# A hybrid decoder trunk on one core: VectorE adds, a plain pair in block 1, stores and adaLN pieces in another order

## The chip, the cores and the metric

The kernel runs on 1 core of one Trainium2 chip. The metric is the device time of one execution in microseconds (us). Before the change it is 2479.21 us, the median of 3 runs (2479.11 to 2483.68). Engines are named as in the profile: PE is TensorE (PEld its weight loads), DVE is VectorE, ACT is ScalarE, POOL is GpSimd, SP is SyncE, which issues the transfers.

## The reference

The kernel computes one inference step of a four-layer trunk for a prompt of 1024 tokens and for 8 samples of 4 tokens, all with width 1024 in float32. Layer 0 and layer 3 are gated short convolutions, layer 1 is an RG-LRU block, layer 2 differential attention. Each layer takes a shift, scale and gate from a conditioning vector (adaLN), and ends with a residual and a LayerNorm. The change touches the two convolution layers and the order of adaLN work:

```python
def adaln(c, w, b):
    m = (jax.nn.silu(c) @ w + b)[:, None, :]
    shift, scale, gate = jnp.split(m, 3, axis=-1)

def short_conv_mixer(u, buf, w_in, conv_w, w_out):
    h, bg, cg, z = jnp.split(u @ w_in, 4, axis=-1)
    y, new_buf = causal_dwconv(cg * h, buf, conv_w)      # width 3
    return (jax.nn.silu(z) * bg * y) @ w_out, new_buf
```

## The kernel before, in words

Prompt and sample tokens stand side by side: NT = 1056 columns, features on the 128 partitions, so an activation is 8 tiles of 128 x 1056. Every float32 operand of a large product is split into a high and a low part (`split`, L93 and L94: ACT casts the high part, DVE subtracts), and a product is three matmuls per block of 128 features. Unit `u[k]` holds both parts of input block k; `y[k]` is where the layer's output will stand, and until then it is used for other things.

The input projection of a convolution layer has four parts (q = 2: cg, 0: h, 3: z, 1: bg), each with 8 column blocks i. `conv_layer` makes them in three ways.

- Block 0 is made plainly, in three chunks of 384, 384 and 288 columns (`part`, with `gemm_chunk`, L124), 24 matmuls a chunk and part. Its results are multiplied, convolved and gated by ACT and DVE, and stored to `yd[0]` by three stores (L496), issued as they are traced.
- Blocks 1 to 7 are made in pairs of two parts: kind 0 is cg and h, kind 1 is z and bg. A pair (`pair`, matmuls at L603) takes seven products of half width instead of eight, 7 x 24 matmuls of 264 columns. It needs sums of the inputs and of the weights. `conv_sums` makes the input sums for four pairs of blocks d: two adds of 128 x 1056 on POOL (L393), which join the high and low part of `u[d]` and `u[d + 4]`, four subtractions of 528 columns on DVE (L397 to L400), and two splits into `y[d]` and `y[d + 4]`. The sums are traced by `more()` between block 0's parts; their tiles come from a ring of three. `conv_pair_weights` makes a pair's weights in six stages: load, direct (a split of the first weight), sums, early, late, last. The stages of the next pair are traced inside the current one; those of the first pair, block 1 kind 0, all ahead of it, after `swap(True)` has closed block 0's pool of temporaries and opened the pool of the fast form.
- The last pair, block 7 kind 1, is plain again (L690, 2 x 4 chunks of 264 columns), with weights from `conv_weights`.

Full plain weights live in a ring of two slots (`wtile`), and the raw loads in another ring of two (`raw`); in layer 0 the fast form has raw tiles of its own. In layer 0 the plain weights of block 0 are slots 1 and 2 of the ring and `y[2]`, `y[3]`; in layer 3 one of them is `y[1]`.

The adaLN projection of a layer is six pieces (`ada_piece`, L186 to L208): four loads of 512 KB into the raw ring, 8 matmuls of 512 columns, an ACT copy, four transposes, two DVE instructions. `filler(s, tot)` traces the pieces that are due at step s: in layer 0 the gate of layer 0 (two pieces) and the six of layer 1, in layer 1 those of layers 2 and 3.

The order on each engine isn't the traced one. A planner runs a simulated time line over the traced program and puts each instruction on its engine when its inputs and memory are ready there; earlier traced instructions go first. Each engine, and the SP queue of transfers, then works through its own list in order.

Of the kernel before, what the change touches and what calls it, by code (L numbers as in the profile page):

```python
# [14 lines left out]
AF = mybir.ActivationFunctionType  # L15
# [30 lines left out]
class Trunk:  # L46
# [340 lines left out]
    def conv_sums(self, l, u, e, d):  # L387
        nc = self.nc
        b = []
        for x in (u[d], u[d + 4]):  # L390
            t = self.xct(f"cs{l}_{d}_{len(b)}")
            xf = x.bitcast(F32)
            nc.gpsimd.tensor_tensor(t, xf[:, :NT], xf[:, NT:], ALU.add)  # L393
            b.append(t)
        (b11, b12), (b21, b22) = ((t[:, :HB], t[:, HB:]) for t in b)
        tt = nc.vector.tensor_tensor
        tt(b11, b12, b11, ALU.subtract)  # L397
        tt(b12, b22, b12, ALU.subtract)
        tt(b22, b22, b11, ALU.subtract)
        tt(b21, b21, b22, ALU.subtract)  # L400
        for t, o in zip(b, (e[d], e[d + 4])):
            self.split((o[:, :NT], o[:, NT:]), t, NT)
# [55 lines left out]
    def conv_layer(self, l, u, y, filler, wts, swap, yd):  # L458
# [10 lines left out]
        def part(i, q, c, wt, cg, yc, sz, p, psv):  # L469
            c0, n = CH[c]  # L470
            npr = min(n, T - c0)
            ps = self.gemm_chunk(wt, u, c, f"in{l}_{i}_{q}_{c}")
            if q == 2:
                cg[c] = cg.get(c) or self.sm(f"cg{l}_{i}_{c}")
                nc.scalar.copy(cg[c][:, :n], ps[:, :n])
            elif q == 0:
                yc[c] = yc.get(c) or self.sm(f"yc{l}_{i}_{c}")
                t = p[c] = self.sm(f"p{l}_{i}_{c}")
                if c == 0:
                    nc.gpsimd.memset(t[:, 0:2], 0.0)  # L480
                else:
                    nc.gpsimd.tensor_copy(t[:, 0:2], p[c - 1][:, 384:386])
                nc.vector.tensor_tensor(t[:, 2 : 2 + npr], ps[:, :npr], cg[c][:, :npr], ALU.mult)
                if npr < n:
                    nc.vector.tensor_tensor(
                        psv[:, :, 2:6], ps[:, npr:n].rearrange("p (b t) -> p b t", b=NB),
                        cg[c][:, npr:n].rearrange("p (b t) -> p b t", b=NB), ALU.mult,
                    )
                conv(i, t, yc[c], psv, npr, n)
            elif q == 3:  # L490
                sz[c] = sz.get(c) or self.sm(f"sz{l}_{i}_{c}")
                nc.scalar.activation(sz[c][:, :n], ps[:, :n], AF.Silu)
            else:
                nc.vector.tensor_tensor(sz[c][:, :n], ps[:, :n], sz[c][:, :n], ALU.mult)
                nc.vector.tensor_tensor(yc[c][:, :n], yc[c][:, :n], sz[c][:, :n], ALU.mult)
                nc.sync.dma_start(yd[i][:, c0 : c0 + n], yc[c][:, :n])  # L496


        def conv(i, t, o, psv, npr, n):
# [20 lines left out]
            return psv  # L520


        sums = [0, 1, 2, 3] if first else [0, 2, 3, 1]

        def more():
# [5 lines left out]
        if first:  # L531
            for s in range(4):
                ld(s)
            for c in range(3):
                for s, q in enumerate((2, 0, 3, 1)):
                    part(0, q, c, wts[s], cg, yc, sz, p, psv)
                    if c == 2:
                        more()
            for s in range(4):
                filler(s, 4 * KB)  # L540
        else:
            for s in range(3):
                ld(s)
            for c in range(3):
                for s, q in enumerate((2, 0)):
                    part(0, q, c, wts[s], cg, yc, sz, p, psv)
            for s in range(2):
                wts.pop(s)
            ld(3)
            for s, q in ((2, 3), (3, 1)):  # L550
                if s == 2:
                    for c in range(3):
                        sz[c] = self.sm(f"sz{l}_0_{c}")
                for c in range(3):
                    more()
                    part(0, q, c, wts[s], cg, yc, sz, p, psv)
        wts.clear()
        swap(True)


# [30 lines left out]
        def pair(i, kind, get, o, stages, fills):  # L591
# [3 lines left out]
            for n, (tgt, mov) in enumerate(steps):  # L595
# [16 lines left out]
                elif n == 2:  # L612
                    u2 = copies(f"u2{nm}", B["X"])
                elif n == 3:
                    p5 = copies(f"p5{nm}", B["Z"])
                elif n == 4:
                    u3 = copies(f"u3{nm}", B["X"])
                    for jj in range(2):
                        nc.gpsimd.tensor_tensor(u3[jj], u3[jj], p5[jj], ALU.add)  # L619
                elif n == 5:  # L620
                    for jj in range(2):
                        nc.vector.tensor_tensor(
                            o[:, HB + QH * jj : HB + QH * jj + QH], B["Z"][jj][:, :QH], u2[jj], ALU.add)
# [3 lines left out]
                    filler(fills.pop(0), 4 * KB)  # L627
            return [t[:, :QH] for t in B["X"]] + u3

        self.deal(tp="Q", mm="U", a="P", b="R")  # L630
        todo = [(i, k) for i in range(1, KB) for k in range(2)][:-1]
        stages, get = self.conv_pair_weights(l, *todo[0], raw)
        for f in stages:
            f()
        yc = None
        for n, (i, kind) in enumerate(todo):
            w2 = {}
            if n + 1 < len(todo):
                stages, nxt = self.conv_pair_weights(l, *todo[n + 1], raw)
            else:  # L640
                def wl(s):
                    return lambda: w2.update({s: self.conv_weights(l, y, s)})
                stages, nxt = [lambda: None, wl(4 * KB - 2), lambda: None, lambda: None, lambda: None, wl(4 * KB - 1)], None
            fills = [4 * i + 2 * kind, 4 * i + 2 * kind + 1]
            if kind == 0:
                t = wide(f"cp{l}_{i}")
                nc.gpsimd.memset(t[:, 0:2], 0.0)
                psv = past(i)
                o = t[:, 2 : NT + 2]
            else:  # L650
                t = wide(f"sz{l}_{i}")
                o = t[:, :NT]
            second = pair(i, kind, get, o, stages, fills)
            if kind == 1:
                for h in range(2):
                    nc.scalar.activation(o[:, HB * h : HB * h + HB], o[:, HB * h : HB * h + HB], AF.Silu)
            for jj, sec in enumerate(second):
                oc = o[:, QH * jj : QH * jj + QH]
                nc.vector.tensor_tensor(oc, sec, oc, ALU.mult)
            if kind == 0:  # L660
                yc = wide(f"yc{l}_{i}")
                nc.gpsimd.tensor_copy(
                    psv[:, :, 2:6], t[:, 2 + T : 2 + NT].rearrange("p (b t) -> p b t", b=NB))
                conv(i, t, yc, psv, T, NT)
            else:
                nc.vector.tensor_tensor(yc[:, :NT], yc[:, :NT], o, ALU.mult)
                nc.sync.dma_start(yd[i], yc[:, :NT])
            get = nxt
# [886 lines left out]
    def run(self):  # L1555
# [17 lines left out]
        def filler_for(*ls):  # L1573
# [4 lines left out]
            total = len(pieces)  # L1578

            def filler(s, tot):  # L1580
                while pieces and (s + 2) * total >= tot * (total - len(pieces) + 1):
                    l, n = pieces.pop(0)
                    self.ada_piece(l, n)
                    if n == 3:
# [182 lines left out]
```

## Time and profile before

| | before |
|---|---|
| time, median of 3 runs | 2479.21 us |
| profiled execution, its own time | 2479.05 us |
| span, first to last instruction | 2477.3 us |
| PE busy | 2364.2 us (95%) |
| DVE busy | 1429.6 us (58%) |
| ACT busy | 998.7 us (40%) |
| POOL busy | 284.0 us (11%) |
| mean granted PE clock | 0.981 |

All rows are from one profiled execution. A busy share is an average over stages with different limits; what a change in one stage is worth is read from that stage, from what PE waits for there. In a timeline row the number in brackets is the engine's idle time ahead of the row's first instruction, with what ended it. In a row of windows each engine has its busy time and its instructions in the order PE, PEld, DVE, ACT, POOL, and then come the granted PE clock (1.00 is full), the share of the DMA engines and GB/s.

### The profile page before, as it was taken

The numbers are of one execution on the slowest core, as the hardware profiler recorded it, in microseconds if no ns is written. First come the engines' busy times: TensorE is split into PE (matmuls) and PEld (weight loads), VectorE is DVE, ScalarE is ACT, GpSimd is POOL, SyncE is SP. The second block draws the span as 40 slices with busy tenths as digits, with TensorE's granted clock in tenths as the row PEclk, the third lists the DMA queues.
The fourth block names the chain that finished last, engine by engine and source line by source line (L and its number), as shares of the span: only waits on it lengthen the run. The fifth ranks groups of instructions, "written<-read, shape, count | busy, mean of one in ns | idle before, by whom it ended". The sixth has DMA issues, their size and how long they took to land.

```text
span 2477.3 us, 44030 instructions
## 1 busy us (share of the span) xinstructions
PE 2364.2 (95%) x16862; PEld 2041.9 (82%) x16862; DVE 1429.6 (58%) x2972; ACT 998.7 (40%) x2059; POOL 284.0 (11%) x384
## 2 busy tenths in 40 slices
PE   7799999999999999999999988888999998999997
PEld 5599999997888897777777966665676998999997
DVE  6865564457466546343333257777784578666555
ACT  4333333336554434122222257667672344333310
POOL 0310000001001000000000023232210022010000
PEclk9899999999999999999999999999999998999999
DMA  9233334423443525254578578889878221222342
GB/s 325 87 95 112 103 111 141 141 83 120 136 133 115 164 70 170 73 160 155 187 271 272 153 209 252 254 239 259 263 245 284 74 92 52 69 61 69 113 132 80
DMA packets 281337, 379.43 MB, mean 153 GB/s; under 512 B 15597, under 2 KB 193902, under 8 KB 281126
## 3 DMA queue, kind: packets, MB, share of 16 engines
q1 hardware_dynamic: 281126, 376.62, 49.2%
q8 instruction: 133, 2.18, 0.4%
q14 instruction: 78, 0.64, 0.1%
HBM read 321.50 MB, written 55.05 MB: 152 GB/s over the span
## 4 chain that ended last, share of the span: by engine, by line
PE 82%; DMA 9%; DVE 5%; ACT 2%; issue 1%; SPq 1%; POOL 0%; DVEq 0%; ACTq 0%; POOLq 0%
PE op L124 15%; PE inX L603 12%; PE qk L1028 10%; PE inZ L603 6%; DMA kp<-cache_k 4%; PE xb L124 4%; PE zz L124 4%; PE z L124 4%; PE skt L1363 4%; PE inY L603 3%; PE ada L192 2%; PE S L1144 2%; PE sps L1344 2%; PE g L860 2%; PE pv L1237 2%; PE sacc L1403 2%
## 5 line engine op out<-in xcount | busy, mean ns | idle before, releaser
L1028 PE MATMUL qk<-wq,ua 128*128 128x512 f32 x1152 | 288.6, 401 | 0.0
L1028 PEld LDWEIGHTS qk<-wq,ua 128*128 128x128 f32 x1152 | 210.7, 188 | 60.0 <-issue 12.5
L1363 PE MATMUL skt<-ident,kp 128*128 128x128 f32 x1024 | 144.3, 277 | 19.5 <-DMA kp<-cache_k 18.0
L1363 PEld LDWEIGHTS skt<-ident,kp 128*128 128x128 f32 x1024 | 116.4, 142 | 46.8 <-issue 16.9
L284 DVE SCALAR_TENSOR_TENSOR r<-op,gate,xr 128x384 f32<-128x384 f32 (+1 forms) x96 | 54.4, 570 | 122.7 <-PE op L124 82.8
L1196 ACT ACTIVATE P<-S,rr 128x512 f32<-128x512 f32 (+2 forms) x192 | 111.0, 585 | 34.5 <-DVE rr L1184 20.7
L1367 DVE COPY sk<-skt 128x512 f32<-128x512 f32 x128 | 86.9, 686 | 63.9 <-PE skt L1363 43.4
L1144 PE MATMUL S<-ks,qhl 128*128 128x512 f32 (+2 forms) x384 | 111.1, 394 | 9.1 <-ACT P L1196 9.0
L1367 ACT COPY sk<-skt 128x512 f32<-128x512 f32 x128 | 75.1, 590 | 80.5 <-PE skt L1363 54.6
L192 PE MATMUL ada<-wada,ct 128*32 128x512 f32 x384 | 87.8, 640 | 19.4 <-DMA wada<-w_ada 18.2
L124 PEld LDWEIGHTS z<-ub,wrz 128*128 128x128 f32 x576 | 92.7, 188 | 11.7 <-issue 10.1
L124 PE MATMUL zz<-ua,wz 128*128 128x384 f32 (+1 forms) x576 | 102.0, 329 | 0.0
L124 PE MATMUL z<-ub,wrz 128*128 128x384 f32 (+1 forms) x576 | 98.3, 326 | 0.0
L124 PEld LDWEIGHTS zz<-ua,wz 128*128 128x128 f32 x576 | 92.2, 188 | 7.1 <-issue 7.0
L619 POOL TENSOR_TENSOR u<-u,p 128x264 f32<-128x264 f32 x52 | 40.4, 779 | 469.3 <-ACT u L586 440.0
L1032 ACT ACTIVATE qkr<-qk 128x512 f32<-128x512 f32 x48 | 28.4, 597 | 157.0 <-PE qk L1028 93.7
L124 PEld LDWEIGHTS xb<-ub,wrx 128*128 128x128 f32 x504 | 81.0, 188 | 12.7 <-issue 9.2
L1403 PE MATMUL sacc<-vp,pt 128*32 128x256 f32 x1024 | 74.1, 396 | 15.0 <-DMA vp<-cache_v 12.8
L124 PE MATMUL xb<-ub,wrx 128*128 128x384 f32 (+1 forms) x504 | 88.0, 328 | 0.0
L124 PE MATMUL op<-ub,ua 128*128 128x384 f32 (+1 forms) x504 | 85.4, 326 | 0.0
L124 PE MATMUL op<-ua,ub 128*128 128x384 f32 (+1 forms) x504 | 85.3, 325 | 0.0
L1237 PEld LDWEIGHTS pv<-V,wt 128*128 128x128 f32 x576 | 75.6, 198 | 10.9 <-issue 2.5
(492 smaller groups left out, 5440.8 us busy)
## 6 DMA issues: line engine op xcount, KB each, us to landing
kp<-cache_k SPq DMA_DIRECT2D x128, 512.0 KB, 4.8
vp<-cache_v SPq DMA_DIRECT2D x128, 512.0 KB, 5.0
wada<-w_ada SPq DMA_DIRECT2D x96, 512.0 KB, 4.2
wra<-a_w_in SPq DMA_DIRECT2D x26, 512.0 KB, 4.1
wrb<-a_w_in SPq DMA_DIRECT2D x26, 512.0 KB, 4.3
xa<-xat SPq DMA_DIRECT2D x64, 192.0 KB, 1.9
xr<-xa SPq DMA_DIRECT2D x64, 192.0 KB, 3.7
tok<-kd SPq DMA_DIRECT2D x32, 256.0 KB, 7.0
```

Of the source, the lines that this page charges most:

```text
L124: nc.tensor.matmul(ps[:, :n], wt[:, wp, k], self.ucols(units[k], up, c), start=i == 0, stop=i == 3 * KB - 1)
L192: nc.tensor.matmul(ps[c : c + 32, :], self.ct[:, k], wts[k // 2][:, k % 2], start=k < 4, stop=k >= 4, tile_position=(0, c),)
L284: nc.vector.scalar_tensor_tensor(r[:, :npr], ps[:, :npr], gate[:, d, 0:1], xt[:, :npr], ALU.mult, ALU.add)
L603: nc.tensor.matmul(B[tgt][jj][:, :QH], w[n][:, wp, k], mov[k](jj, up), start=new and m == 0, stop=m == 11, skip_group_check=not new)
L860: nc.tensor.matmul(ps[:, :n], wt[:, wp, q, k, m * 128 : (m + 1) * 128], self.ucols(y[2 * i + k], up, c), start=j == 0, stop=j == 5,)
L1028: nc.tensor.matmul(ps, u[k][:, c0 : c0 + 128], wq[n, k // 2][:, wp, k % 2], start=i == 0, stop=i == 3 * KB - 1)
L1144: nc.tensor.matmul(st[:, o : o + w], qs[h, g][:, part, s, 128 * qj : 128 * qj + 128], ks[h][:, s, l0 : l0 + w], start=part == 0, stop=part ...
L1196: nc.scalar.activation(p[:, o : o + w], x["S"][s][i][:, :w], AF.Exp, scale=-1.0, bias=rr[:, 6 + s : 7 + s], accum_out=rr[:, c : c + 1])
L1237: nc.tensor.matmul(x["pv"], x["w"][kb // 4][:, j : j + 128], V[h][:, kb], start=kb == 0, stop=kb == qb)
L1363: nc.tensor.transpose(tp[:, 128 * g : 128 * g + 128], pg[j][:, 128 * h : 128 * h + 128], ident)
L1367: e(kt[:, :, 128 * j : 128 * j + 128], tp.rearrange("p (g t) -> p g t", g=4))
L1403: nc.tensor.matmul(acc[32 * g : 32 * g + 32, :], pts[0][:, 128 * (p % 4) + 32 * g : 128 * (p % 4) + 32 * g + 32], v[:, 256 * g : 256 * g + ...
```

## The change

The input sums' adds (L393) and the add of two partial products inside a fast pair (L619) go from POOL to DVE. Block 0's three stores are kept in a list `late` and issued after the first fast pair's loads. Block 1 kind 0 becomes a plain pair: `w2` loads its two weights before the pools are swapped, `plain` makes 2 x 4 chunks of 24 matmuls of 264 columns, and inside it the stages of the next pair, block 1 kind 1, are traced by `step`, one after each chunk of the second half (direct, sums, early, late; last comes behind). The fast pairs start with block 1 kind 1. The filler after block 0 is gone, and a call of the filler traces at most one piece (`if` for `while`), so that the first two pieces of layer 0 are traced inside the pair (1,1), at its steps 2 and 5.

```diff
--- before.py
+++ after.py
@@ -390,7 +390,7 @@
         for x in (u[d], u[d + 4]):
             t = self.xct(f"cs{l}_{d}_{len(b)}")
             xf = x.bitcast(F32)
-            nc.gpsimd.tensor_tensor(t, xf[:, :NT], xf[:, NT:], ALU.add)
+            nc.vector.tensor_tensor(t, xf[:, :NT], xf[:, NT:], ALU.add)
             b.append(t)
         (b11, b12), (b21, b22) = ((t[:, :HB], t[:, HB:]) for t in b)
         tt = nc.vector.tensor_tensor
@@ -493,7 +493,7 @@
             else:
                 nc.vector.tensor_tensor(sz[c][:, :n], ps[:, :n], sz[c][:, :n], ALU.mult)
                 nc.vector.tensor_tensor(yc[c][:, :n], yc[c][:, :n], sz[c][:, :n], ALU.mult)
-                nc.sync.dma_start(yd[i][:, c0 : c0 + n], yc[c][:, :n])
+                late.append((yd[i][:, c0 : c0 + n], yc[c][:, :n]))
 
 
         def conv(i, t, o, psv, npr, n):
@@ -520,6 +520,7 @@
             return psv
 
 
+        late = []
         sums = [0, 1, 2, 3] if first else [0, 2, 3, 1]
 
         def more():
@@ -536,8 +537,6 @@
                     part(0, q, c, wts[s], cg, yc, sz, p, psv)
                     if c == 2:
                         more()
-            for s in range(4):
-                filler(s, 4 * KB)
         else:
             for s in range(3):
                 ld(s)
@@ -554,7 +553,7 @@
                 for c in range(3):
                     more()
                     part(0, q, c, wts[s], cg, yc, sz, p, psv)
-        wts.clear()
+        w2 = {s: self.conv_weights(l, y, s) for s in (4, 5)}
         swap(True)
 
 
@@ -616,7 +615,7 @@
                 elif n == 4:
                     u3 = copies(f"u3{nm}", B["X"])
                     for jj in range(2):
-                        nc.gpsimd.tensor_tensor(u3[jj], u3[jj], p5[jj], ALU.add)
+                        nc.vector.tensor_tensor(u3[jj], u3[jj], p5[jj], ALU.add)
                 elif n == 5:
                     for jj in range(2):
                         nc.vector.tensor_tensor(
@@ -627,42 +626,76 @@
                     filler(fills.pop(0), 4 * KB)
             return [t[:, :QH] for t in B["X"]] + u3
 
-        self.deal(tp="Q", mm="U", a="P", b="R")
-        todo = [(i, k) for i in range(1, KB) for k in range(2)][:-1]
-        stages, get = self.conv_pair_weights(l, *todo[0], raw)
-        for f in stages:
-            f()
-        yc = None
-        for n, (i, kind) in enumerate(todo):
-            w2 = {}
-            if n + 1 < len(todo):
-                stages, nxt = self.conv_pair_weights(l, *todo[n + 1], raw)
-            else:
-                def wl(s):
-                    return lambda: w2.update({s: self.conv_weights(l, y, s)})
-                stages, nxt = [lambda: None, wl(4 * KB - 2), lambda: None, lambda: None, lambda: None, wl(4 * KB - 1)], None
-            fills = [4 * i + 2 * kind, 4 * i + 2 * kind + 1]
-            if kind == 0:
-                t = wide(f"cp{l}_{i}")
-                nc.gpsimd.memset(t[:, 0:2], 0.0)
-                psv = past(i)
-                o = t[:, 2 : NT + 2]
-            else:
-                t = wide(f"sz{l}_{i}")
-                o = t[:, :NT]
-            second = pair(i, kind, get, o, stages, fills)
+
+        def plain(i, kind, o, w2, step):
+            for s in (0, 1):
+                for c in range(4):
+                    oc = o[:, QH * c : QH * c + QH]
+                    ps = self.mm(f"in{l}_{i}_{kind}_{s}_{c}")
+                    m = 0
+                    for k in range(KB):
+                        for wp, up in ((0, 0), (0, 1), (1, 0)):
+                            nc.tensor.matmul(
+                                ps[:, :QH], w2[4 * i + 2 * kind + s][:, wp, k],
+                                u[k][:, up * NT + QH * c : up * NT + QH * c + QH], start=m == 0, stop=m == 3 * KB - 1)
+                            m += 1
+                    if s == 1:
+                        nc.vector.tensor_tensor(oc, ps[:, :QH], oc, ALU.mult)
+                    elif kind == 0:
+                        nc.scalar.copy(oc, ps[:, :QH])
+                    else:
+                        nc.scalar.activation(oc, ps[:, :QH], AF.Silu)
+                    step(s, c)
+
+
+        def conv_in(i, run):
+            t = wide(f"cp{l}_{i}")
+            nc.gpsimd.memset(t[:, 0:2], 0.0)
+            psv = past(i)
+            run(t[:, 2 : NT + 2])
+            yc = wide(f"yc{l}_{i}")
+            nc.gpsimd.tensor_copy(psv[:, :, 2:6], t[:, 2 + T : 2 + NT].rearrange("p (b t) -> p b t", b=NB))
+            conv(i, t, yc, psv, T, NT)
+            return yc
+
+        def fast(i, kind, get, o, stages):
+            second = pair(i, kind, get, o, stages, [4 * i + 2 * kind, 4 * i + 2 * kind + 1])
             if kind == 1:
                 for h in range(2):
                     nc.scalar.activation(o[:, HB * h : HB * h + HB], o[:, HB * h : HB * h + HB], AF.Silu)
             for jj, sec in enumerate(second):
                 oc = o[:, QH * jj : QH * jj + QH]
                 nc.vector.tensor_tensor(oc, sec, oc, ALU.mult)
+
+        todo = [(i, k) for i in range(1, KB) for k in range(2)][1:-1]
+        stages, get = self.conv_pair_weights(l, *todo[0], raw)
+        stages.pop(0)()
+        for dst, src in late:
+            nc.sync.dma_start(dst, src)
+
+        def step(s, c):
+            if stages and (s, c) in ((1, 0), (1, 1), (1, 2), (1, 3)):
+                stages.pop(0)()
+
+        self.deal(tp="QU", mm="PR")
+        yc = conv_in(1, lambda o: plain(1, 0, o, w2, step))
+        for f in stages:
+            f()
+        self.deal(tp="Q", mm="U", a="P", b="R")
+        w2 = {}
+        for n, (i, kind) in enumerate(todo):
+            if n + 1 < len(todo):
+                stages, nxt = self.conv_pair_weights(l, *todo[n + 1], raw)
+            else:
+                def wl(s):
+                    return lambda: w2.update({s: self.conv_weights(l, y, s)})
+                nop = lambda: None
+                stages, nxt = [nop, wl(4 * KB - 2), nop, nop, nop, wl(4 * KB - 1)], None
             if kind == 0:
-                yc = wide(f"yc{l}_{i}")
-                nc.gpsimd.tensor_copy(
-                    psv[:, :, 2:6], t[:, 2 + T : 2 + NT].rearrange("p (b t) -> p b t", b=NB))
-                conv(i, t, yc, psv, T, NT)
+                yc = conv_in(i, lambda o: fast(i, kind, get, o, stages))
             else:
+                o = wide(f"sz{l}_{i}")[:, :NT]
+                fast(i, kind, get, o, stages)
                 nc.vector.tensor_tensor(yc[:, :NT], yc[:, :NT], o, ALU.mult)
                 nc.sync.dma_start(yd[i], yc[:, :NT])
             get = nxt
@@ -1578,7 +1611,7 @@
             total = len(pieces)
 
             def filler(s, tot):
-                while pieces and (s + 2) * total >= tot * (total - len(pieces) + 1):
+                if pieces and (s + 2) * total >= tot * (total - len(pieces) + 1):
                     l, n = pieces.pop(0)
                     self.ada_piece(l, n)
                     if n == 3:
```

## Rows read from the trace of the kernel before

**Rows 1.** The page: its first line, and PE's line of part 1.

```profile
span 2477.3 us, 44030 instructions
...
PE 2364.2 (95%) x16862; PEld 2041.9 (82%) x16862; DVE 1429.6 (58%) x2972; ACT 998.7 (40%) x2059; POOL 284.0 (11%) x384
```

**Rows 2.** Timeline of PE, layer 0 (start us, us, engine, line, operation, tile, [idle before]).

```profile
84.90 6.51 PE L124 MATMUL in<-ua,ub 128*128 128x288 f32 x48
...
108.35 1.92 PE L192 MATMUL ada<-wada,ct 128*32 128x512 f32 x4 [10.32 <-DMA wada<-w_ada]
...
117.22 0.75 PE L603 MATMUL inY<-ua,wa 128*128 128x264 f32 x4 [0.95 <-ACT wa L413]
```

**Rows 3.** Windows of layer 0, cut at pair starts (us; per engine busy; clock; DMA).

```profile
91.40:117.20 25.80, 9.74 (x29) 1.56 (x28) 17.41 (x24) 6.63 (x8) 8.58 (x7) 0.60 0.46 132
...
138.25:160.06 21.81, 21.81 (x181) 20.84 (x180) 13.51 (x22) 9.42 (x18) 1.74 (x4) 1.00 0.34 98
...
160.06:180.49 20.43, 20.43 (x170) 20.43 (x169) 12.44 (x22) 6.69 (x14) 2.37 (x5) 1.00 0.25 78
...
180.49:204.91 24.42, 24.42 (x190) 21.49 (x189) 13.44 (x22) 9.42 (x18) 1.80 (x4) 1.00 0.42 132
```

**Rows 4.** Timeline of PE, layer 3, end of the first block.

```profile
2045.36 4.74 PE L124 MATMUL in<-ua,ub1b 128*128 128x288 f32 x24 [2.40 <-ACT cg L475]
...
2052.96 11.52 PE L124 MATMUL in<-ua,wi 128*128 128x384 f32 x70 [2.02 <-DVE wi L109]
...
2076.50 1.25 PE L603 MATMUL inX<-ub1a,wsS 128*128 128x264 f32 x4 [6.66 <-ACT wsS L413]
```

**Rows 5.** Windows of layer 3, the second one up to a pair's start.

```profile
2069.80:2076.50 6.70, 0.04 (x2) 0.00 (x1) 5.51 (x10) 2.61 (x6) 0.00 (x0) 0.68 0.06 22
...
2076.50:2093.87 17.37, 17.37 (x121) 17.37 (x121) 12.81 (x22) 6.98 (x14) 2.79 (x5) 0.83 0.22 62
```

**Rows 6.** Timeline of the SP queue, layer 0.

```profile
92.43 0.38 SPq L186 DMA_DIRECT2D wada<-w_ada  x1
...
103.91 0.32 SPq L496 DMA_DIRECT2D yd<-yc  x1
...
110.77 0.42 SPq L425 DMA_DIRECT2D wra<-a_w_in  x1
```

**Rows 7.** Timeline of DVE, layer 3: a weight split, the last sum split.

```profile
2052.97 1.21 DVE L414 TENSOR_TENSOR wa<-wra,wa 128x1024 fp32r<-128x1024 f32 x1
...
2073.94 1.26 DVE L94 TENSOR_TENSOR ub1a<-cs,ub1a 128x1056 fp32r<-128x1056 f32 x1 [1.19 <-ACT ub1a L93]
```

**Rows 8.** Lines L393 and L619 on POOL (ns least/median/most, first and last start).

```profile
L393 POOL TENSOR_TENSOR cs<-ua x8: 2400/2690/3484, 59.5 to 101.2; 128x1056 f32<-128x1056 f32 x8
...
L619 POOL TENSOR_TENSOR u<-u,p x52: 746/753/1209, 132.9 to 2334.0; 128x264 f32<-128x264 f32 x52
```

**Rows 9.** Groups of DVE, 59 to 109 us (count, busy us, mean ns, idle before).

```profile
L94 DVE TENSOR_TENSOR ub<-cs,ub 128x1056 fp32r<-128x1056 f32 x8 | 9.9, 1248 | 0.0
...
L94 DVE TENSOR_TENSOR ua<-u,ua 128x288 fp32r<-128x288 f32 x8 | 7.2, 906 | 0.4 <-ACT ua L93 0.4
...
L399 DVE TENSOR_TENSOR cs<-cs,cs 128x528 f32<-128x528 f32 x4 | 6.8, 1696 | 0.1
...
L397 DVE TENSOR_TENSOR cs<-cs 128x528 f32<-128x528 f32 x4 | 5.1, 1267 | 0.0
...
L503 DVE SCALAR_TENSOR_TENSOR yc<-p,pv,yc 128x384 f32<-128x384 f32 x2 | 3.4, 1723 | 0.0
...
L398 DVE TENSOR_TENSOR cs<-cs,cs 128x528 f32<-128x528 f32 x4 | 2.8, 698 | 0.0
...
L495 DVE TENSOR_TENSOR yc<-yc,sz 128x288 f32<-128x288 f32 x1 | 2.3, 2330 | 0.0
```

**Rows 10.** Timeline of PE, layer 3, last pair of columns (192 plain matmuls).

```profile
2339.23 23.50 PE L690 MATMUL in<-ua,wi 128*128 128x264 f32 x192
```

**Rows 11.** Timeline of DVE, layer 0: the last two sum splits.

```profile
105.91 2.53 DVE L94 TENSOR_TENSOR ub<-cs,ub 128x1056 fp32r<-128x1056 f32 x2
```

## The prediction

> **What bounds the kernel now.** I read the page first, for the span and PE's share of it. Outside the span lie 2479.05 - 2477.3 = 1.75 us [rows 1]; the sum below starts from the profiled execution's 2479.05, 0.16 below the median of the runs (2479.21). PE is busy 95% of the span [rows 1], so a change pays only where PE waits, where it runs below full clock, or where its own work changes. The edits touch the two convolution layers alone, so I went to PE's timeline there. In layer 0 the first block's last matmul ends at 84.90 + 6.51 = 91.4, and the first seven-product pair, block 1 kind 0, starts at 117.2 [rows 2]. In between PE has an adaLN piece and a half, fed by slow loads (one wait of 10.32 [rows 2]). The window shows it busy for 9.74 of 25.80 us at a granted clock of 0.60, a mix of the two levels, 1.2 and 2.4 GHz [rows 3]. From then on pairs follow one another without a hole: 20.43 us for a pair, 24.42 for one with an adaLN piece in it, so a piece costs 3.99 [rows 3]. In layer 3 the same place has waits of 2.40, 2.02 and 6.66 [rows 4], and a clock of 0.68, then 0.83 [rows 5].
>
> Why the first pair is late in layer 0 stands in the SP queue: its weights are loaded at 110.77, behind adaLN loads and behind the last store of the first block, which goes at 103.91 [rows 6]. In layer 3 it is VectorE: PE waits 6.66 for the split of the weight sums [rows 4], and VectorE works on the input sums until 2073.94 + 1.26 = 2075.2 [rows 7].
>
> **The change, part by part.**
>
> 1. *Input adds from POOL to VectorE.* POOL makes eight adds a layer of 128x1056, 2.69 us each [rows 8]. VectorE takes them. Their price on that engine isn't in the trace; the nearest row has the same shape and two SBUF inputs, the split's subtraction at 1.25 [rows 9], so I take 8 x 1.25 = 10.0. Bounds for one add: 1.25 below, POOL's 2.69 above. What VectorE gets back: equal work takes very unequal times now. A 528-column subtraction is 0.70 in line 398 but 1.70 in line 399 and 1.27 in line 397: 4 x 1.00 + 4 x 0.57 = 6.3 us of stretch. At line 398's 1.32 ns a column, the 288-column split should take about 0.4 instead of 0.91 (8 x 0.5 = 4.0), line 495 0.4 instead of 2.33 (1.9), line 503 0.5 instead of 1.72 (2 x 1.2 = 2.4) [rows 9]. Together some 14 us in layer 0, while POOL is adding. So the move gives VectorE back about 14 - 10 = 4 us.
> These rows show an instruction of 0.70 at 1.70 on average beside POOL's adds [rows 8, 9]. The Trainium skill, SBUF - State Buffer, section Who interferes with whom, says why: the two engines take a shared port pair as an exclusive lock, and whichever comes second waits for the whole of the other's instruction. By that rule each add could hold VectorE for its full 2.69, 21.5 us a layer, and VectorE would get 7 us more back; the measured 14 is used.
>
> 2. *One more plain pair.* Block 1 kind 0 becomes 8 x 24 = 192 plain matmuls instead of 7 x 24 = 168. The trace has just this: 192 of 264 columns in 23.50 [rows 10], against the pair's 20.43. So +3.1 us of PE a layer, and in these 23.5 us the next pair's weights can be loaded, summed and split beside PE. What is late next is the plain pair's own first weight: it needs a slot of the two-slot ring, an ACT copy and a VectorE subtraction (wa's took 1.21 [rows 7]).
>
> When does VectorE get to that subtraction? It is issued behind all input sums. In layer 0 their last splits end at 105.91 + 2.53 = 108.4 [rows 11]. After the change VectorE's whole list ends at about 108.4 - 14 + 10 + 2.4 (two new splits) = 106.8, so the first split, if it comes last but one, ends at 105.6. The lower bound for the plain pair's start is 91.4, the end of the first block. Layer 3 shows what the planner does with a split issued that late: wa's runs at 2052.97, 22 us before the last sum's end [rows 7], so it slips into holes. With the adds on VectorE the holes are fewer. I take 96, a third of the way from 91.4 to 105.6.
>
> 3. *Layer 0.* Milestone: the start of block 2's first pair, before at 160.06 [rows 3]. After: 96 + 1.5 (PE restarts at a lower clock) + 23.5 + the pair (1,1), 20.43, with two adaLN pieces, 2 x 3.99 = 149.4. Gain 10.6. The pieces: before, one and a half lay in the stall and PE paid 21.81 - 20.43 = 1.4 for the rest [rows 3]; after, both lie in the pair, so 6.6 of the stall's 25.8 isn't won. With a start at 91.4 the gain is 160.06 - 143.3 = 16.7; with 105.6 and 2.8 for the clock it is -0.3. The 2.8 is from layer 3: after 6.7 idle, 121 matmuls took 17.37 [rows 5] where they should take 14.5 at the pair's 20.43/170 = 0.120 [rows 3]. 1.5 is about half, for an idle time of 4.6.
>
> 4. *Layer 3.* Milestone: the start of pair (1,1), before at 2093.87 [rows 5]. The first block ends at 2052.96 + 11.52 = 2064.5 [rows 4]. Two waits before that hang on VectorE, or on ACT queued behind it (2.40 and 2.02 [rows 4]); I take half as gone, so 2062.3, and 0.9 for the weight's split: 2063.2. Then 2063.2 + 23.5 = 2086.7, a gain of 7.2. Bounds: both waits gone and the split on time, 2060.1 + 23.5, a gain of 10.3; the split behind all sums, 2075.2 - 14 + 10 + 1.2, less 3.3 of the fast pair's weight work that now comes after (wa's 1.21 and three of 0.7), = 2069.1, with 2.8 for the clock 2095.4, a loss of 1.5. The stretch is taken as in layer 0.
>
> 5. *Stores behind the loads.* Three stores a layer leave their place ahead of the pair's loads on SP; in layer 0 the last held the queue until 103.91 [rows 6]. The loads' new time costs PE nothing: the fast weights are due at 96 + 25 = 121, and from issue to first matmul it took 117.2 - 110.8 = 6.4 [rows 2, 6]. Behind the stores now queue the adaLN loads and block 2's weights, due 20 us later. Should the loads wait for the memory of the closed pool, whose last reader is that store, 104 + 6.4 is still in time; if that cover is gone, it costs what they come beyond 121.
>
> 6. *adaLN pieces one by one*: one at each of two fill points instead of two at the first; their 2 x 3.99 is in step 3. *POOL's small adds* (0.75 us, 52 of them [rows 8]) to VectorE: they lie beside pairs where PE is busy 20.43 of 20.43 and VectorE 12.44 [rows 3]. Nothing; without that cover two of 0.7 a pair.
>
> Sum: 2479.05 - 10.6 - 7.2 = 2461.2.
>
> **The rivals.**
> *Weights on time in both layers*: gains of 16.7 and 9, so 2453. For it: wa's early split [rows 7]. Against: VectorE is busy 17.41 of 25.80 in the stall itself [rows 3], and the sums come first.
> *The stall moves rather than goes*: the split comes near the end of the sums (101 and 2065), or (1,1) waits for its own weights as long. Layer 0: 101 + 2.8 + 51.9 = 155.7, gain 4.4; layer 3: 2065 + 1.5 + 23.5 = 2090, gain 3.9; so 2471. For it: an in-order VectorE that is full. Against: in layer 0 PE waited for a load, not for VectorE [rows 2].
> *Slower: VectorE becomes the bound.* The eight adds cost more than 1.25 there, and the plain pair's first split waits behind them. It decides from starts of 105.3 (160.06 - 2.8 - 23.5 - 28.4) and 2067.6 on; each us beyond costs one per layer. At 1.95 an add, halfway to POOL's 2.69, the latest starts become 111.2 and 2074.7, layer 0 loses 5.9 and layer 3 7.1: 2492. Against it: the row of the same shape at 1.25 [rows 9].
> The Trainium skill speaks for this rival: Perfetto Trace Analysis, section Optimizing Scalar/DVE Operations, would take work off a saturated VectorE, to ScalarE or POOL, though it doubts the latter as those two share a port. The stretch in [rows 9] bears out the doubt.
> *It does nothing*: what is won and the extra 3.1 balance, within 0.2%, which is 5.0 us and about what a measurement of this kernel can tell from no change.
>
> **How the numbers follow.** Forecast 0.40 (2456 to 2466), on time 0.24, moved stall 0.25 (a tenth of it within 5 us of before), nothing 0.05, slower 0.06. Faster by over 0.2% (below 2474.2): 0.40 + 0.24 + 0.22 = 0.86. Within: 0.08. Slower: 0.06. The range of 8 in 10 goes from 2450, a little under the on-time case for waits that I did not count, to 2474, the upper end of the moved stall. An add's price is in it at 1.25 and a little over; at POOL's price it isn't.
>
> **What would show it.** In the trace after: no adds of 1056 columns on POOL, and lines 397 and 399 at 0.70 like line 398. Block 1's plain matmuls start between 91.4 and 101 in layer 0, and last 23.5. No wait ahead of (1,1), which takes about 28.4 with two adaLN pieces; block 2's first pair starts at 149 instead of 160. In layer 3 the plain pair starts within 2 us of the first block's end. It would be wrong if PE waits for the new weight's subtraction beyond 101, if (1,1) waits for its weight sums, if SP holds block 2's loads behind a store or a raw slot, or if the later layers' order moves by more than 3 us.

## The result, and the profile after

The changed kernel takes 2450.66 us (median of 4 runs, 2444.07 to 2452.47) against 2480.92 (4 runs, 2479.11 to 2483.68) for the kernel before: a ratio of 0.9872, with a 95% interval of 0.9851 to 0.9894. It is faster by 30 us; 18 were forecast. At this ratio the 2479.21 us that the prediction started from become 2447.5, just below its range of 2450 to 2474. The profiled execution is the longest of the four: 2452.47, with a span of 2450.6.

The page of the changed kernel, its first line and PE's, DVE's and POOL's lines of part 1 [rows 1]:

```profile
span 2450.6 us, 43997 instructions
...
PE 2360.8 (96%) x16910; PEld 2042.6 (83%) x16910; DVE 1420.9 (58%) x3012; ACT 991.5 (40%) x2043; POOL 207.8 (8%) x316
```

VectorE took over the adds and is busy for less time than before, 1420.9 instead of 1429.6 us.

PE's timeline after, layer 0 (start, us, engine, line, tile, count) [rows 2]:

```profile
85.00 6.50 PE L124 MATMUL in<-ua,ub 128*128 128x288 f32 x48
91.34 17.66 PE L638 MATMUL in<-ua,wi 128*128 128x264 f32 x144
108.93 1.06 PE L192 MATMUL ada<-wada,ct 128*32 128x512 f32 x8
109.93 6.11 PE L638 MATMUL in<-ua,wi 128*128 128x264 f32 x48
115.88 0.65 PE L602 MATMUL inY<-ua,wa 128*128 128x264 f32 x4
```

No row has a wait in brackets. The plain pair (line 638) begins where the first block ends, and the fast pair (1,1) follows without a hole.

Windows after, cut at the starts of the plain pair, (1,1), (2,0) and (2,1) [rows 3] (us; then PE, PEld, DVE, ACT and POOL busy; clock; DMA share and rate):

```profile
91.34:115.88 24.54, 24.54 (x203) 23.56 (x201) 18.70 (x27) 6.49 (x9) 5.76 (x2) 1.00 0.35 112
115.88:139.19 23.31, 23.31 (x191) 21.36 (x189) 17.27 (x32) 11.58 (x22) 2.05 (x5) 1.00 0.37 109
139.19:162.46 23.27, 23.27 (x183) 21.30 (x182) 13.59 (x26) 7.28 (x15) 0.87 (x3) 1.00 0.43 142
```

PE is busy for the whole of each window at full clock. (2,1) starts at 162.46 instead of 180.49 with the same two adaLN pieces done: 18.0 us won. (Block 2's first pair, the prediction's milestone, starts at 139.19 instead of 160.06, but half an adaLN piece is still to come there, so the next start is the one to compare.)

DVE's timeline after, in the same stretch:

```profile
78.82 1.25 DVE L393 TENSOR_TENSOR cs<-ua 128x1056 f32<-128x1056 f32 x1
...
84.50 1.22 DVE L109 TENSOR_TENSOR wi<-wi_2r,wi 128x1024 fp32r<-128x1024 f32 x1
...
88.47 1.22 DVE L109 TENSOR_TENSOR wi<-wi_0r,wi 128x1024 fp32r<-128x1024 f32 x1
89.60 1.26 DVE L393 TENSOR_TENSOR cs<-ua 128x1056 f32<-128x1056 f32 x1
...
103.49 2.49 DVE L94 TENSOR_TENSOR ub<-cs,ub 128x1056 fp32r<-128x1056 f32 x2
```

These rows decide the case. Both weight splits of the plain pair (line 109) are done by 89.7, before PE needs them and with input adds still to come behind them. The last sum split ends at 103.49 + 2.49 = 106.0.

Layer 3 after: PE's timeline at the end of the first block [rows 4], and the two windows up to (1,1), from layer 3's first matmul on [rows 5]:

```profile
2030.90 0.64 PE L638 MATMUL in<-ua,wi 128*128 128x264 f32 x4
2032.35 11.56 PE L124 MATMUL in<-ua,wi 128*128 128x384 f32 x70 [0.81 <-ACT sz L492]
2043.75 22.99 PE L638 MATMUL in<-ua,wi 128*128 128x264 f32 x188
2066.59 3.08 PE L602 MATMUL inY<-ua,wa 128*128 128x264 f32 x24
```

```profile
1990.04:2043.75 53.71, 52.67 (x329) 50.45 (x327) 43.73 (x91) 23.73 (x39) 5.00 (x10) 1.00 0.16 50
2043.75:2066.59 22.84, 22.84 (x191) 22.84 (x190) 17.98 (x26) 8.74 (x13) 0.00 (x0) 1.00 0.18 55
```

The same two windows of the kernel before, cut at its own starts:

```profile
2005.72:2064.50 58.78, 54.36 (x331) 51.79 (x329) 51.78 (x88) 23.98 (x40) 25.35 (x17) 0.97 0.11 33
2064.50:2093.87 29.37, 22.71 (x165) 22.50 (x164) 23.58 (x36) 11.54 (x21) 5.13 (x7) 0.83 0.18 56
```

88.15 us became 76.55. The first block is 5.1 shorter: 1.04 of idle time is left of 4.42, and PE's own work in it takes 52.67 instead of 54.36 at a clock of 1.00 instead of 0.97. The rest, 6.5, comes out of the second window: the wait of 6.66 ahead of the sums is gone, and PE's work takes 22.84 instead of 22.71, though there is more of it, since the clock is 1.00 instead of 0.83.

To see where the whole execution changed I cut each profiled span at four marks: the first matmul of the kept-rows outputs of layers 0, 1 and 3 (line 365 in the changed kernel; each follows a layer's input projection or scan), and layer 3's first matmul.

| us | layer 0 to its rows | to layer 1's rows | to layer 3's first matmul | to layer 3's rows | rest | span |
|---|---|---|---|---|---|---|
| before | 432.5 | 362.5 | 1210.7 | 356.9 | 114.7 | 2477.3 |
| after | 414.5 | 360.5 | 1215.0 | 345.5 | 115.1 | 2450.6 |
| adds back on POOL | 419.1 | 360.8 | 1207.8 | 352.0 | 115.0 | 2454.7 |
| before, adds on VectorE | 431.7 | 360.3 | 1210.1 | 353.3 | 115.3 | 2470.7 |
| plain splits last | 429.6 | 363.7 | 1206.0 | 356.6 | 114.9 | 2470.8 |
| adds made twice | 425.6 | 360.5 | 1200.4 | 351.8 | 114.9 | 2453.2 |
| stores inline | 414.1 | 360.8 | 1203.8 | 345.5 | 115.1 | 2439.3 |
| two pieces at once | 417.5 | 360.1 | 1205.2 | 345.5 | 115.1 | 2443.4 |
| small add on POOL | 415.6 | 360.5 | 1209.1 | 345.5 | 115.1 | 2445.8 |
| adaLN in fours | 407.1 | 350.1 | 1204.3 | 345.5 | 115.0 | 2422.0 |

The two convolution columns give 18.0 + 11.4 = 29.4, close to the difference of the medians (30.3). In this profile 2.7 of it is hidden, since the middle stretch happened to be 4.3 longer. That stretch varies from one execution to the next (last section), so each experiment is read from the convolution columns as well as from its median.

### The profile page after: what moved, and what is told of

Its sections match the earlier page's. It is cut to its first block, busy times and chain, and to the rows that moved or that the text cites. A ratio compares the mean times of both kernels' runs of the same rounds, so it can differ in the third digit from the quotient of the medians.

```text
span 2450.6 us, 43997 instructions
## 1 busy us (share of the span) xinstructions
PE 2360.8 (96%) x16910; PEld 2042.6 (83%) x16910; DVE 1420.9 (58%) x3012; ACT 991.5 (40%) x2043; POOL 207.8 (8%) x316
## 4 chain that ended last, share of the span: by engine, by line
PE 85%; DMA 9%; DVE 2%; ACT 1%; issue 1%; SPq 0%; POOL 0%; DVEq 0%; ACTq 0%; POOLq 0%
PE op L124 15%; PE inX L602 12%; PE qk L1061 10%; PE inZ L602 6%; DMA kp<-cache_k 5%; PE xb L124 4%; PE skt L1396 4%; PE z L124 4%; PE in L124 4%; PE zz L124 3%; PE inY L602 3%; PE ada L192 3%; DMA vp<-cache_v 2%; PE in L723 2%; PE in L638 2%; PE g L893 2%
## 5 line engine op out<-in xcount | busy, mean ns | idle before, releaser
L1270 PE MATMUL pv<-V,wt 128*128 128x128 f32 x576 | 82.0, 281 | 2.6 <-ACT wt L1262 2.6
```

Of the source, the lines that this page charges most:

```text
L1270: nc.tensor.matmul(x["pv"], x["w"][kb // 4][:, j : j + 128], V[h][:, kb], start=kb == 0, stop=kb == qb)
```

## The experiments

The prediction's mechanism, which the first four test, is that PE wins the stall ahead of the first fast pair, less 3.1 us for the plain pair, if VectorE splits the plain weights in time, and that the adds on VectorE help it to. Each text below states its own theory A and its rivals. The first four kernels ran on one chip beside 19 runs of the kernel before (median 2478.11), the last four on another beside 11 (2478.82). The changed kernel was not run again beside them, so a loss against it is read from the two ratios to the kernel before, which tell it to some 7 us.

**1. Adds back on POOL.** The changed kernel, with the plain pair kept:

```diff
-            nc.vector.tensor_tensor(t, xf[:, :NT], xf[:, NT:], ALU.add)
+            nc.gpsimd.tensor_tensor(t, xf[:, :NT], xf[:, NT:], ALU.add)
...
-                        nc.vector.tensor_tensor(u3[jj], u3[jj], p5[jj], ALU.add)
+                        nc.gpsimd.tensor_tensor(u3[jj], u3[jj], p5[jj], ALU.add)
```

> The changed kernel with both kinds of adds back on POOL; plain pair, filler and stores stay. Theory A (the plain pair covers the stall, the adds only set when its first weight is split and whether layer 3's first block waits): the first new split comes at about 94 instead of 84.5 in layer 0, so PE waits 2 to 4 us there, and layer 3's first block gets its waits back (about 5 us); together 8 us over the changed kernel, about 2459. Rival B (the adds are the gain, the plain pair only exchanges a stall for 3.1 us of work): over 2470.

Measured: 2456.02 (2454.82 to 2457.23, 4 runs), ratio 0.9908 (0.9891 to 0.9924). Against the changed kernel's ratio that is a loss of 9 us, and 4.6 + 6.5 in the convolution columns: theory A holds, and rival B is out. PE's and VectorE's timelines show what comes back in layer 0:

```profile
93.47 24.86 PE L638 MATMUL in<-ua,wi 128*128 128x264 f32 x190 [2.43 <-DVE wi L109]
```

```profile
82.58 2.91 DVE L399 TENSOR_TENSOR cs<-cs,cs 128x528 f32<-128x528 f32 x1
...
92.21 1.21 DVE L109 TENSOR_TENSOR wi<-wi_2r,wi 128x1024 fp32r<-128x1024 f32 x1
```

The split comes at 92.21 instead of 84.50, and a subtraction of line 399 takes 2.91 again. The wait is 2.43 of the 4.6; the 190 matmuls behind it run at a clock of 0.93, and both adaLN pieces that follow cost 4.0.

In layer 3 the first block has its waits of 2.4 (ACT's `cg`) and 2.6 (the split of its own last weight) again, and takes 60.16 instead of 53.71. The plain pair alone wins 13.4 in layer 0 and 4.9 in layer 3.

**2. Adds alone.** The kernel before, with the two adds on VectorE and nothing else (the diff of experiment 1 the other way round).

> The kernel before with both kinds of adds on VectorE and nothing else. Theory A: in layer 0 the fast weights' load still sits behind the adaLN loads and the last store, so the pair starts only some 5 us sooner; in layer 3 the input sums end early, the waits of 2.40, 2.02 and 6.66 mostly go, 10 to 13 us. Together about 2462. Rival B: 2455 or less, since VectorE was what all waited for. Rival C (the adds alone do little, the stall stays until a plain pair covers it): over 2472.

Measured: 2472.24 (2465.89 to 2474.59, 10 runs), ratio 0.9970 (0.9957 to 0.9984). My theory made this far too big; rival C, that the adds alone do little, is right. PE's timeline in layers 0 and 3:

```profile
96.03 3.24 PE L192 MATMUL ada<-wada,ct 128*32 128x512 f32 x8 [3.77 <-DMA wada<-w_ada]
...
119.15 1.25 PE L603 MATMUL inY<-ua,wa 128*128 128x264 f32 x4 [0.94 <-ACT wa L413]
...
2069.84 1.25 PE L603 MATMUL inX<-ub1a,wsS 128*128 128x264 f32 x4 [8.56 <-ACT wsS L413]
```

The first fast pair starts at 119.15, no sooner than at 117.22 [rows 2], since adaLN's loads and its own weights hold it. In layer 3 the first block ends earlier, and the wait for the sums grows from 6.66 [rows 4] to 8.56. Alone the adds win 0.8 and 3.6. Together the two edits win more than their sum: 18.0 against 14.2 in layer 0, 11.4 against 8.5 in layer 3. Layer 0's column wanders by some 2 us from one execution to the next (experiment 6), so its 0.8 isn't told apart from nothing, and its surplus is rough. The kernel before without the filler after block 0, whose loads stand ahead of the pair's weights on SP [rows 6], was not run. So how the 13.4 of layer 0 are shared between the plain pair and the filler's going is open; layer 3 has no filler there, and its 4.9 are the plain pair's.

**3. Plain splits last.** The changed kernel, with both splits of the plain weights ordered behind the last sum split, which is where the prediction's upper bound put them (the edit's last part; the others only keep hold of the two instructions):

```diff
...
-        w2 = {s: self.conv_weights(l, y, s) for s in (4, 5)}
+        w2 = {}
+        for s in (4, 5):
+            w2[s] = self.conv_weights(l, y, s)
+            self.after(self.last_sub, self.last_sum)
```

> The changed kernel with one order edge more: the two new splits of the plain pair's weights come behind the last input-sum split on VectorE, which is where the prediction feared them. Theory A (the start of the plain pair moves the time one to one): in layer 0 the first split ends at about 105 instead of 85.7, PE waits 13.6 us from 91.4 and 0 to 2.8 for the clock; in layer 3 about 9.5 and as much for the clock; 23 to 28 us over the changed kernel, 2474 to 2479, all of the gain gone. Rival B (what comes later, the next pair's weights, would have been late anyway): under 10 us over the changed kernel.

Measured: 2470.47 (2467.19 to 2477.85, 10 runs), ratio 0.9970 (0.9959 to 0.9982). The convolution layers lose 15.1 + 11.1 = 26.2 against the changed kernel, as theory A has it, and by the ratios the loss is 24 us; rival B's under 10 is out. PE in layer 0, and DVE:

```profile
105.15 23.77 PE L642 MATMUL in<-ua,wi 128*128 128x264 f32 x180 [12.37 <-DVE wi L109]
```

```profile
101.48 2.48 DVE L94 TENSOR_TENSOR ub<-cs,ub 128x1056 fp32r<-128x1056 f32 x2
103.87 1.22 DVE L109 TENSOR_TENSOR wi<-wi_2r,wi 128x1024 fp32r<-128x1024 f32 x1
```

PE goes on at 105.15, the end of that split; the prediction's upper bound was 105.6. With the split there the prediction's sum has gains of -0.3 and -1.5 over the kernel before; the columns have 2.9 and 0.3. So the sum's mechanism was right, and its price to some 3 us. What was wrong is where the split comes to stand.

**4. Adds made twice.** The changed kernel, with each input add issued a second time on VectorE (a line repeated; the result is overwritten by the same values).

> The changed kernel with each of the eight input adds of a layer made twice on VectorE (the same sum again, 8 x 1.17 us more a layer). Theory A (VectorE has slack of about 9 us under the plain pair): the first new split still ends before 91.4, the sums end at about 115 and the pair (1,1) waits 0 to 2 us in layer 0 and 0 to 1 in layer 3: 0 to 3 us over the changed kernel. Rival B (VectorE is the bound from the first block to the pair, as in the prediction's slower case): each us costs one a layer, 19 us over the changed kernel, about 2469.

Measured: 2457.60 (2454.58 to 2460.26, 4 runs), ratio 0.9918 (0.9901 to 0.9934). The convolution layers lose 11.1 + 6.3 = 17.4, near the rival's 19; by the ratios the loss is 11 us. Theory A's 0 to 3 is out. PE's timeline shows where 10 us more of VectorE come out:

```profile
91.56 17.68 PE L639 MATMUL in<-ua,wi 128*128 128x264 f32 x144
...
113.98 3.24 PE L192 MATMUL ada<-wada,ct 128*32 128x512 f32 x8 [3.74 <-DMA wada<-w_ada]
...
122.71 6.09 PE L639 MATMUL in<-ua,wi 128*128 128x264 f32 x48
...
130.45 0.76 PE L603 MATMUL inY<-ua,wa 128*128 128x264 f32 x4 [1.65 <-ACT wa L414]
...
2061.01 8.51 PE L639 MATMUL in<-ua,wi 128*128 128x264 f32 x48 [4.57 <-ACT cp L646]
```

The plain pair still starts on time (91.56). In layer 0 the stall has moved into its second half, where more adaLN work, fed by loads, stands ahead of its last 48 matmuls. VectorE's own time isn't what runs out there (7.20 of 13.53 us busy from 109.18 to 122.71): it waits for a cast of ACT, which stands in ACT's list behind the copy of that adaLN piece, and the copy waits for PE. Rows of DVE and ACT in this kernel:

```profile
118.86 1.26 DVE L94 TENSOR_TENSOR ub<-cs,ub 128x1056 fp32r<-128x1056 f32 x1 [5.88 <-ACT ub L93]
```

```profile
117.27 0.59 ACT L197 COPY adaev<-ada 128x512 f32<-128x512 f32 x1 [8.98 <-PE ada L192]
```

So in layer 0 the cost comes with the order that the planner made of the longer list, and not from VectorE's time alone; that it is near the rival's 9.5 is chance. In layer 3 PE waits 4.57 ahead of the same 48, behind ACT's copy out of an earlier chunk, which stands behind the casts of the sums; VectorE is busy for 28.78 of the 31.28 us up to 2061.01. There its list is nearly full, as the rival has it.

**5. Stores inline.** The changed kernel, with the first block's stores issued as before:

```diff
-                late.append((yd[i][:, c0 : c0 + n], yc[c][:, :n]))
+                nc.sync.dma_start(yd[i][:, c0 : c0 + n], yc[c][:, :n])
```

> The changed kernel with the first block's stores issued as they are traced, as before. Theory A (the edit of the stores does nothing, since the planner orders the transfers by when they are ready): as the changed kernel, 2450.7 us, within 0.3%. Rival B (the stores behind the loads bring the plain pair's or the first fast pair's weights earlier): 2456 us or more, layer 0's projection ending some 6 us later.

Measured: 2444.63 (2441.15 to 2448.08, 4 runs), ratio 0.9862 (0.9829 to 0.9895); layer 0 and 3 as in after, within 0.4. All five engines have the same instructions in the same order in both programs: this edit did nothing. The SP queue of the changed kernel shows it [rows 6]:

```profile
82.82 0.32 SPq L674 DMA_DIRECT2D yd<-yc  x1
...
99.16 0.34 SPq L674 DMA_DIRECT2D yd<-yc  x1
101.53 0.37 SPq L425 DMA_DIRECT2D wra<-a_w_in  x1
```

The stores are traced behind the loads and still go ahead of them, since the planner places a transfer when its data and memory are ready.

**6. Two pieces at once.** The changed kernel, with the filler's `if` back to `while`.

> The changed kernel with the adaLN pieces traced as before, all that are due at one fill point. Theory A (a piece costs the same wherever it lies, and block 1 has two of them in either way): as the changed kernel, within 0.3%. Rival B (two pieces at one point hold both raw slots and PE waits for loads): layer 0's projection ends 4 us or more later.

Measured: 2446.54 (2441.71 to 2452.91, 4 runs), ratio 0.9869 (0.9834 to 0.9904). By the time, no gain or loss can be told. Layer 0 ends 3.0 later, though PE waits for no load. 1.9 of it is there when the plain pair starts (93.24 instead of 91.34), and up to there all engines work through the same instructions in the same order: in this execution PE's clock fell to its lower level, 1.2 GHz, after a stretch with longer waits (1.41 of 2.00 us busy from 48 to 50, against 1.71 in after), where it stays at 1.00 in after.

```profile
50.00:52.00 2.00, 2.00 (x8) 2.00 (x8) 1.84 (x3) 2.00 (x4) 0.00 (x0) 0.50 0.28 88
```

So layer 0's column wanders by some 2 us by itself. The other 1.1 is one set of four adaLN matmuls that stands apart as two and two (experiment 8).

**7. Small add on POOL.** The changed kernel, with the add of line 618 back on POOL.

> The changed kernel with the small add inside a fast pair (52 of 0.75 us before) back on POOL. Theory A (PE works without a hole beside them): as the changed kernel, within 0.3%. Rival B (VectorE is short of time in the pairs or POOL's adds slow it): 5 us or more either way, spread over both convolution layers.

Measured: 2448.20 (2445.64 to 2448.87, 4 runs), ratio 0.9870 (0.9837 to 0.9902). Layer 0 ends 1.1 later, with one wait of PE that after doesn't have, 1.64 for an adaLN load at 407.68; layer 3 takes as long. Theory A holds: PE never waits for these adds. So nearly all of experiment 1's loss is that of the 16 large adds, as far as the two moves don't act on each other.

**8. adaLN in fours.** This one is not about the cause: PE's rows above show eight records of adaLN's 32-column matmuls in 1.06 us (four matmuls of two records), and elsewhere in the same timeline four records (two matmuls) in 1.05:

```profile
141.47 1.05 PE L192 MATMUL ada<-wada,ct 128*32 128x512 f32 x4
```

The edit puts the matmuls of two loads one behind another:

```diff
-            if first and k0 % 4 == 0:
+            if k0 % 4 == 0:
                 continue
-            for k in range(k0 - 2 if first else k0, k0 + 2):
+            lead = None
+            for k in range(k0 - 2, k0 + 2) if first else (k0, k0 + 1, k0 - 2, k0 - 1):
...
+                if lead and not first:
+                    self.after(mm, lead)
+                lead = mm
```

> The changed kernel, with the four adaLN matmuls of two neighbouring loads put one behind another (layer 0's first four pieces already are). In the trace of the changed kernel four such matmuls take 1.06 us together, and two take 1.05; some 23 times in layers 0 and 1 two and two stand apart. Theory A (PE works without a hole there, so what a piece gets cheaper is won): 23 x 1.05 = 24 us, so about 2427 us against the changed kernel's 2450.7; layer 0's projection ends some 8 us earlier, layer 1 some 15. Rival B (the raw slots are held until both loads are there, and the next weights come late): what is won is lost in waits for loads, 2445 us or more.

Measured: 2425.40 (2418.34 to 2432.17, 6 runs), ratio 0.9782 (0.9754 to 0.9810). It beats both kernels; against the three kernels above that ran beside it, 2444.6 to 2448.2, by some 19 to 23 us. The group of these matmuls in after, and the same group in this kernel:

```profile
L192 PE MATMUL ada<-wada,ct 128*32 128x512 f32 x384 | 83.4, 623 | 3.5 <-DMA wada<-w_ada 2.4 <-ACT ct L152 1.0
```

```profile
L193 PE MATMUL ada<-wada,ct 128*32 128x512 f32 x384 | 59.7, 627 | 6.2 <-DMA wada<-w_ada 5.1 <-ACT ct L152 1.0
```

The work shrinks by 23.7 us, as expected. Of that, layer 0 wins 7.4 (8 expected) and layer 1 10.4 (15 expected). In layer 1 PE is busy 13.6 less (355.8 to 342.2) and idle 3.2 more; the longest new wait is 1.50, for an adaLN load. The rival's cost is real there, and small.

## Why the prediction was right in direction and short in size

*The failed step* is in part 2: "With the adds on VectorE the holes are fewer. I take 96". The split stood at 84.50 and the plain pair began at 91.34, the lower bound. In layer 3 it stood at 2030.77, 13 us ahead of the pair's start. I had worked from the end of VectorE's whole list, which gave 105.6, and gone a third of the way there. The list's end was right (106.0 measured; 106.8 forecast), but a list's end doesn't tell where one item stands. ACT's timeline has the cast of that weight's high part:

```profile
82.55 1.05 ACT L108 CAST wi<-wi_2r 128x1024 fp32r<-128x1024 f32 x1
```

It is ready at 82.55 + 1.05 = 83.6, and VectorE takes the split at 84.50, one subtraction later, while each later input sum is still a chain of add, subtraction, cast and split. The row that showed this was already cited: `wa`'s split 22 us ahead of the last sum [rows 7]. I read it as a split that needs a hole, and discounted it for fewer holes; no hole is needed: VectorE works without a pause around 84.50. Experiment 3 confirms the reading by forcing the split to the end: PE then goes on at 105.15. Nor does the split need the adds on VectorE to come early: in experiment 1 it runs at 92.21, 18 us ahead of the last sum split's end (110.7).

*Layer 0*, 18.0 for 10.6, by the forecast's own terms: 96 - 91.34 = 4.7; the 1.5 for a slower clock, since PE never idles and the clock stays at 1.00; and 1.2 for the pieces, which cost 71.12 - 23.5 - 2 x 20.43 = 6.8 and not 8.0 (71.12 is from 91.34 to 162.46): the first of the two now has both its sets of four matmuls whole, which saves 1.05 (experiment 8). Together 7.4, the whole miss.

*Layer 3*, 11.4 for 7.2. I took half of 2.40 + 2.02 as gone; three quarters of it went, and the clock it had cost came back too, so the first block is 5.1 shorter instead of 2.2. The 0.9 for the split wasn't paid. The plain pair's window is 0.7 shorter than 23.5, since four of its 192 matmuls run ahead of it, at 2030.90, where PE would otherwise wait. Together some 4.4, about the miss (4.2 by the columns).

*The rival "weights on time in both layers"* (2453, chance 0.24) is what happened: 18.0 and 11.4 against its 16.7 and 9. That I put the sums first was my argument against it, and it is the part that failed.

*What held.* The add costs 1.25 on VectorE, between 1.245 and 1.258 over all 16:

```profile
L393 DVE TENSOR_TENSOR cs<-ua x16: 1245/1252/1258, 60.5 to 2047.2; 128x1056 f32<-128x1056 f32 x16
```

What VectorE got back is there as well [rows 9]: groups of DVE after, 59 to 110 us.

```profile
L94 DVE TENSOR_TENSOR ua<-u,ua 128x288 fp32r<-128x288 f32 x8 | 3.6, 455 | 2.1 <-ACT ua L93 2.1
...
L399 DVE TENSOR_TENSOR cs<-cs,cs 128x528 f32<-128x528 f32 x4 | 2.8, 703 | 0.0
...
L397 DVE TENSOR_TENSOR cs<-cs 128x528 f32<-128x528 f32 x4 | 2.8, 701 | 0.0
```

Lines 397 and 399 are at 0.70, like line 398. The plain pair takes 24.54 with one half of an adaLN piece (1.00) in it: 23.5. Block 2's pairs follow without a wait. The small adds cost nothing. The slower rival falls by the 1.25. The Trainium skill's advice that spoke for it (Perfetto Trace Analysis, section Optimizing Scalar/DVE Operations) is to take work off a saturated VectorE, with a doubt where POOL takes it. The doubt is borne out here: experiment 1 took the adds off VectorE, to POOL, and lost 4.6 + 6.5 us in the two layers.

*What was said of the stores* (part 5) failed as a description and cost nothing: they didn't move. The fast weights were loaded at 101.5, ahead of their due time.

## What to carry to other kernels

When a planner or a ready-first queue sets the order, ask when an instruction's inputs are ready and what stands before it then, not when its engine's whole list ends; if the nearest row shows such an instruction done early, take that as the likeliest place. Price two edits together where one's gain needs the other: here each alone won 0.8 and 13.4 in layer 0, both 18.0. And before a stall is hunted, look whether the same instruction has two prices in one timeline: the adaLN matmuls did, and regrouping them was worth some 20 us more, beside the change's 30.

## What the runs showed of the hardware that I had not expected

- *The middle stretch wanders by itself.* After and "stores inline" have the same instructions in the same order, yet from layer 1's rows to layer 3's first matmul they took 1215.0 and 1203.8 us. Most of it lies in the part from the first score matmul on, where PE waits for cache loads: 572.64 and 563.89, with DMA busy for 0.77 and 0.76 of the time. Of these 8.7 us PE is idle for 5.2 and busy for 3.5; why isn't shown, and the two executions were not side by side. A single profile of this kernel can't tell 10 us of gain there from none.
- *POOL pays too.* With VectorE working back to back, a POOL copy of 128 x 16 that takes 0.20 elsewhere (median of 16) took 5.66, all of it beside VectorE's sums, and 5.66 again in experiment 7. POOL's timeline after, layer 0:

```profile
96.48 5.66 POOL L519 COPY psv<-pv 128x16 f32<-128x16 f32 x1 [5.42 <-DVE yc L510]
```

  In [rows 8, 9] VectorE's instructions are stretched beside POOL's; this is the same in the other direction. Nothing on PE waited for that copy.
- *Four column groups cost what two do.* Eight records of 128*32 adaLN matmuls on four column groups take 1.06 us, four on two groups 1.05; with all in fours 23.7 us of PE's work went.
